# Scan of an RWKV-7 layer: the next front is begun in the chain's first step, its copies, exponents and grams queued behind the merge and the first solutions

## The chip, the cores and the metric

The kernel runs on one core of a Trainium2 chip. The metric is the time of one execution on the device in microseconds (us), the median over several runs. A profiled execution of the same kernel gives the trace.

The engines named below are TensorE (PE, matrix multiplications; PEld is its load of weights), VectorE (DVE), ScalarE (ACT), GpSimd (POOL) and SyncE (SP), which issues the DMAs. Each engine takes its instructions in the order of its own queue and waits where an operand or a buffer isn't ready.

## The reference

Two layers run over 256 context tokens and 512 latent tokens with 1024 features. Layer 0 is windowed attention with an MLP. Layer 1 is an RWKV-7 mixer with an MLP. The change lies in the mixer's scan: for each of 16 heads of 64 features, in both directions, a state of 64 by 64 runs over the tokens; the latent scan begins with the context's last state.

```python
def wkv_scan(r, w, k, v, a, b, s0, reverse):
    def step(s, inp):
        r_t, w_t, k_t, v_t, a_t, b_t = inp
        sa = jnp.einsum('bhvk,bhk->bhv', s, a_t)
        s = s * w_t[:, :, None, :] + sa[..., None] * b_t[:, :, None, :] + v_t[..., None] * k_t[:, :, None, :]
        return s, jnp.einsum('bhvk,bhk->bhv', s, r_t)
...
    _, y_fwd = wkv_scan(r, dec[0], k, v, na, b, s_fwd, False)
    _, y_bwd = wkv_scan(r, dec[1], k, v, na, b, s_bwd, True)
```

## The kernel before

Attention, the two MLPs and the features of the RWKV layer are matrix products split in high and low parts (lines 334 to 366 and their callers); the change doesn't touch them. The features (kk, bp, kp, r, the running sums of the log decay and the gates) are written to memory by tiles of 128 features, and the scan reads them back.

**Items.** `rwkv_scan` cuts the scan into six items (`its`, `plan`). Item 0 is the context of feature tiles 0 to 3 (four tiles, 4 chunks of 64 tokens), items 1 and 2 are the latent tokens of tiles 0, 1 and 2, 3 (two tiles, 8 chunks each); items 3, 4, 5 are the same for tiles 4 to 7. A chunk of one head and one direction is a triangular system of 64 unknowns. Each item goes through these stages:

- **The front**, `prep` (L1153): for each feature tile `fl` and direction `d` it loads the features (`load`, L1184, and the decay sums `cs`, L1197; L1165 to L1174 for a context item), takes two exponents on ScalarE (`en`, L1200, and `cs` in place, L1201; L1177 and L1178 for a context item), and forms the scaled operands by three or four products on DVE (L1213 to L1217). GpSimd copies the decay over a chunk (`PC`, L1218). The buffers: five for the features (`f4`), two for the sums (`cs`, NCS), one for `en` (NEN). Then `grams` (L1223), for four chunks at a time: ScalarE copies the operand into one of two padded tiles (L1235), TensorE makes four products (L1238) in one of two PSUM buffers, DVE masks the result into GM (L1244). One front has eight such grams, called simply grams below.
- **The lanes**, `lanes` (L1278): the diagonal blocks of 32 by 32 are copied from GM to MT (L1284, by `copy`, two on ScalarE at L1263, two on DVE at L1267, by FC), transposed into `lane` (L1285), and inverted by elimination, 30 steps of products and sums on DVE (L1295, L1298). This is a serial chain on one engine.
- **The merge**, `merge` (L1300): the inverse is transposed back twice (L1303 and L1306, both DVE), TensorE makes the off-diagonal block in two stages of 32 by 32 products (L1313, L1321), each in two halves with its evacuation on ScalarE (L1316, L1324), and four copies (L1329, by BC two on ScalarE and two on DVE) put the diagonal blocks in GM.
- **Late work**, `late` (L1247): for a latent item the second half of the grams, for each item the scaling to the chunk's end (L1259) and the transposed operands (`turn`, L1331), done part by part in the steps of the chain before.
- **The chain**, `chain` (L1359): over the chunks in order, in two groups of tiles: x = GM z plus the state's part (L1382, L1385), evacuated to `xsb` on ScalarE (L1390); the solution U = GM xsb (L1397), evacuated to `z` (L1401); the new state (L1412, DVE L1417 for the first, L1423 after); for a latent item the output (L1433, L1437, L1439). After each step `after` loads a later chunk's values, does late work and a piece of the last item's `readout` (L1445).

**Order.** The kernel is written for a scheduler that gives each engine's queue its order at build time: it goes by the order in which the program issues its instructions as a priority, and by the times at which operands and buffers are expected, so that later work can be queued first where earlier work isn't ready. `tc.issue_after(i)` is a fixed order: what the block issues on the engine of instruction `i` stands behind `i` in that engine's queue; other engines aren't bound, and nothing waits on data by it. Before the change, `front(n)` merges item n-1, issues the front of item n with its DVE instructions behind the merge's second transposition (`back`, L1306), and the lanes of item n; then the chain of item n-1 is issued. So the front and the lanes of the next item come ahead of the chain in the program, and beside it in time. The front of the item after that can be loaded, and its first exponents taken, as soon as buffers are free.

Of the kernel before, what the change touches and what calls it, by code (L numbers as in the profile page):

```python
# [11 lines left out]
AF = mybir.ActivationFunctionType  # L12
# [128 lines left out]
LS = (0, 0, 1, 1, 1, 1, 1, 0)  # L141
LC = (0, 2, 4, 4)
NCS = 2
NEN = 1
SQ = ()
LM = ()
LPRE = 0
# [10 lines left out]
RW = {'rt': 'tile'}  # L158
DM = (0, 0, 2, 3, 3, 3, 3, 2)
FC = 'avav'  # L160
BC = 'avav'
TD = ((1, 3),)
NG = 2
NTM = 7
# [6 lines left out]
class K:  # L171
# [909 lines left out]
    def rwkv_scan(self, xsave, osave):  # L1081
# [8 lines left out]
        rl, _ = rconst_layout()  # L1090
# [59 lines left out]
            it.zw = {}  # L1150
            return it

        def prep(it):  # L1153

            it.AR, it.BK, it.GM = ABG[it.set]
            it.PC = sa.tile([P, it.nch, it.nf, 2], F32, tag="pc", bufs=2, name="pc")
# [28 lines left out]
                    src[fl, nm] = t.rearrange("p (c t) -> p c t", t=64)  # L1185

            def part(fl, d):
                if d == 0:
                    load(fl)
                f = it.fts[fl]  # L1190
                b = slice(fl * it.nch, fl * it.nch + it.nch)
                kk, bp, kp = (src[fl, nm] for nm in ("kk", "bp", "kp"))
                inc = slice(1 - d, 65 - d)
                exc = slice(d, 64 + d)
                if it.lat:
                    cs = ftile(it.nch * 65, "cs", NCS, "cs")
                    nc.sync.dma_start(cs, self.fslice(f, f"L{d}", 65 * 4, it.nch * 65))  # L1197
                    cs = cs.rearrange("p (c t) -> p c t", t=65)
                    en = ftile(n, "en", NEN, "en").rearrange("p (c t) -> p c t", t=64)
                    nc.scalar.activation(en, cs[:, :, inc], AF.Exp, scale=self.DEC)  # L1200
                    nc.scalar.activation(cs, cs, AF.Exp, scale=-self.DEC)  # L1201
                else:
                    cs, en = src[fl, d]
                    en = en[:, :, inc]
                ep = cs
                ar, bk = it.AR[:, d, b], it.BK[:, d, b]
                if d == 0:
                    ao, bo, ko = ar[:, :, 0:64], bk[:, :, 0:64], bk[:, :, 64:128]
                    ends = ep[:, :, 64]
                else:  # L1210
                    ao, bo, ko = ar[:, :, 0:64][:, :, ::-1], bk[:, :, 64:128][:, :, ::-1], bk[:, :, 0:64]
                    ends = ep[:, ::-1, 0]
                nc.vector.tensor_tensor(ko, kp, en, ALU.mult)  # L1213
                nc.vector.tensor_tensor(bo, bp, en, ALU.mult)
                nc.vector.tensor_tensor(ao, kk, ep[:, :, exc], ALU.mult)
                if it.lat:
                    nc.vector.tensor_tensor(ar[:, :, 64:128], src[fl, "r"], ep[:, :, inc], ALU.mult)  # L1217
                nc.gpsimd.tensor_scalar(it.PC[:, :, fl, d], ends, 1.0, 0.0, ALU.mult, ALU.add)  # L1218
                grams(it, fl, d, 0)

            return [lambda fl=fl, d=d: part(fl, d) for fl in range(it.nf) for d in range(2)]

# [38 lines left out]
        def copy(eng, o, i):  # L1261
            if eng == "a":
                nc.scalar.activation(o, i, AF.Copy)  # L1263
            elif eng == "p":
                nc.gpsimd.tensor_scalar(o, i, 1.0, 0.0, ALU.mult, ALU.add)
            else:
                nc.vector.tensor_copy(o, i)  # L1267

        def streams(s_):

# [29 lines left out]
        def merge(it):  # L1300
# [2 lines left out]
            nc.vector.transpose(MT.rearrange("p u i -> p i u"), Lt.rearrange("p t s -> p s t"))  # L1303

            DT = dt if it.n else GM[:, 0, :, 64:96]
            it.back = nc.vector.transpose(DT.rearrange("p u t -> p t u"), lane).ins  # L1306
            R = [slice(64 * d, 64 * d + 32) for d in range(2)]
            Q = [slice(64 * d + 32, 64 * d + 64) for d in range(2)]
            for u0 in (0, 16):
# [7 lines left out]
            for u0 in (0, 16):  # L1317
# [3 lines left out]
                        nc.tensor.matmul(ps[R[d], 32 * u:32 * u + 32], MT[Q[d], u0 + u], DT[Q[d], u0 + u],  # L1321
                                         start=True, stop=True, tile_position=(64 * d + 32, 64 * d))
                for d in range(2):
                    nc.scalar.activation(GM[R[d], d, u0:u0 + 16, 32:64], ps[R[d]].rearrange("p (u i) -> p u i", u=16),  # L1324
                                         AF.Copy)
            for j in range(4):
                d, bk_ = j // 2, j % 2
                r = slice(32 * j, 32 * j + 32)
                copy(BC[j], GM[r, d, :, 32 * bk_:32 * bk_ + 32], DT[r])  # L1329

        def turn(it):  # L1331

# [26 lines left out]
        def chain(it, S_, after):  # L1359
# [6 lines left out]
            for i in range(nch):  # L1366
                hpr = tc.high_priority(HP) if HP else ExitStack()
                with hpr:
# [22 lines left out]
                    for g in range(NG):  # L1391
                        hs = range(hg * g, hg * g + hg)
                        gs = slice(hg * g, hg * g + hg)
                        for hd in hs:
                            for d in range(2):
                                o = slice(64 * d, 64 * d + 64)
                                nc.tensor.matmul(UP[o, 64 * hd:64 * hd + 64], GM[:, d, it.cof(i, d) * nh + hd, 0:64], xsb[:, d, hd],  # L1397
                                                 start=True, stop=True, tile_position=(0, 64 * d))
                        for d in range(2):
                            o = slice(64 * d, 64 * d + 64)  # L1400
                            nc.scalar.activation(Z[o, d, gs], UP[o, 64 * hg * g:64 * hg * g + 64 * hg].rearrange(  # L1401
# [147 lines left out]
                return [state[0][:, f:f + 2]]  # L1549
            return [state[f // 2][:, 0:1], state[f // 2][:, 1:2]]  # L1550

        def front(n):
            merge(its[n - 1])

            with tc.issue_after(its[n - 1].back):
                for p in prep(its[n]):
                    p()
            lanes(its[n])
            rest.extend(late(its[n]))
            for _ in range(LPRE):  # L1560
                if rest:
                    rest.pop(0)()

        tail = {}

# [51 lines left out]
            return r  # L1617

        pending, rest = [], []
        front(1)  # L1620
        for n, it in enumerate(its):
            def after(i):
                if i % it.spb == it.spb - 1:
                    lookahead()
                for _ in range(lper if n == len(its) - 1 else (LS if it.lat else LC)[i]):
# [17 lines left out]
            for p in pending + rest:  # L1643
                p()
            rest.clear()
            if n + 2 < len(its):
                front(n + 2)
            elif n + 1 < len(its):
                merge(its[n + 1])
            pending = readout(it) if it.lat else []  # L1650
            if not it.lat:
# [126 lines left out]
```

## Time and profile before

| | us |
|---|---|
| median of 3 runs | 2264.61 (2261.82 to 2271.43) |
| the profiled execution | 2270.0 |
| its span, first to last instruction | 2268.2 |
| from the first merge to the last (L1303) | 1372.5 to 1766.3 |
| from merge to merge | 90.7, 74.8, 75.6, 81.7, 71.0 |
| the last chain, with the output projection beside it | from 1766.3, to about 1852 |

The page gives busy times of the engines over the whole span. The granted clock of TensorE is a mean of 0.944 over it. A row of the timeline has the start in us from the span's first instruction, the duration, the engine, the line, the operation, what it writes and reads, and in brackets the idle time of the engine before it and what ended that. A row with x2 or more stands for that many instructions in a row. The number of a matmul row counts each product twice.

### The profile page before, as it was taken

To read this page: it belongs to the slowest core of one execution; us is meant where nothing else is said; L and a number is where in the kernel's file an instruction comes from. 1 tells how busy PE (TensorE), PEld (TensorE's weight loads), DVE (VectorE), ACT (ScalarE), POOL (GpSimd) and SP (SyncE) were. 2 spreads that over 40 slices of the span, in tenths; PEclk is the share of its full clock that TensorE was granted. 3 is DMA by queue.
4 is the path that set the end of the run, shared out by engine and by line. 5 is a ranking of instruction groups with operands and counts; after the bars stand their busy time and mean duration, and the time that the engine had idled before them with its cause. 6 is when DMAs were issued, how large, how long until landed. Compare 5 with 4: busy or idle time off the path is not lost. (4 is left out here: it accounts for less than half of the span.)

```text
span 2268.2 us, 40460 instructions
## 1 busy us (share of the span) xinstructions
PE 2049.9 (90%) x16208; PEld 1668.3 (74%) x16208; DVE 1320.1 (58%) x2737; ACT 857.2 (38%) x1702; POOL 263.7 (12%) x362
## 2 busy tenths in 40 slices
PE   5989999979999999997979798698869887999999
PEld 4876756868888888885856687586658655787887
DVE  4465565464334343349787665888898657444443
ACT  4344454232111111116454445567647433222121
POOL 0122232010000000001010101000000101101110
PEclk9999999989999999997999898789889898999999
DMA  8344461122122121116146434113311312323322
GB/s 288 102 135 135 138 212 58 56 79 65 61 61 66 56 70 61 53 37 236 63 162 244 135 129 155 35 51 90 95 48 58 128 56 79 103 93 95 96 88 80
DMA packets 115885, 229.67 MB, mean 101 GB/s; under 512 B 12912, under 2 KB 31088, under 8 KB 115312
## 3 DMA queue, kind: packets, MB, share of 16 engines
q1 hardware_dynamic: 115696, 227.08, 31.1%
q8 instruction: 128, 2.10, 0.4%
q14 instruction: 61, 0.50, 0.1%
HBM read 191.80 MB, written 32.60 MB: 99 GB/s over the span
## 5 line engine op out<-in xcount | busy, mean ns | idle before, releaser
L337 DVE TENSOR_TENSOR wlo<-wraw,whi 128x1024 fp32r<-128x1024 f32 (+1 forms) x121 | 134.5, 1120 | 322.6 <-ACT whi L334 169.2
L364 PE MATMUL w_ps<-mhl,whi 128*128 128x512 f32 (+1 forms) x768 | 235.7, 361 | 7.3 <-DVE mhl L317 7.3
L362 PE MATMUL w_ps<-mhh,whi 128*128 128x512 f32 (+1 forms) x768 | 235.1, 361 | 7.1 <-POOL whi L336 3.4
L366 PE MATMUL w_ps<-mhh,wlo 128*128 128x512 f32 (+1 forms) x768 | 235.4, 361 | 5.0 <-DVE wlo L337 5.0
L364 PE MATMUL w_ps<-hid,w2h 128*128 128x512 f32 (+1 forms) x768 | 234.0, 359 | 0.0
L362 PE MATMUL w_ps<-hid,w2h 128*128 128x512 f32 (+1 forms) x768 | 231.4, 355 | 1.6 <-ACT mrelu L689 1.4
L366 PE MATMUL w_ps<-hid,w2l 128*128 128x512 f32 (+1 forms) x768 | 231.1, 355 | 0.0
L334 ACT ACTIVATE w2h<-w2raw 128x512 fp32r<-128x512 f32 x64 | 40.4, 631 | 330.0 <-PE w_ps L364 299.1
L660 DVE SCALAR_TENSOR_TENSOR X<-w_ps,ada,X 128x256 f32<-128x256 f32 (+1 forms) x128 | 73.1, 612 | 137.5 <-PE w_ps L366 137.5
L364 PEld LDWEIGHTS w_ps<-mhl,whi 128*128 128x128 f32 x768 | 127.7, 190 | 33.0 <-DVE mhl L317 9.8
L362 PEld LDWEIGHTS w_ps<-mhh,whi 128*128 128x128 f32 x768 | 127.8, 190 | 31.7 <-POOL whi L336 4.1
L366 PEld LDWEIGHTS w_ps<-mhh,wlo 128*128 128x128 f32 x768 | 127.8, 190 | 31.0 <-DVE wlo L337 8.0
L336 POOL TENSOR_SCALAR whi<-wraw 128x1024 fp32r<-128x1024 f32 (+1 forms) x60 | 69.2, 1154 | 673.2 <-PE w_ps L364 252.6
L366 PEld LDWEIGHTS w_ps<-hid,w2l 128*128 128x128 f32 x768 | 127.4, 189 | 23.3
L362 PEld LDWEIGHTS w_ps<-hid,w2h 128*128 128x128 f32 x768 | 125.5, 188 | 24.8 <-ACT mrelu L689 2.3
L334 ACT ACTIVATE whi<-wraw 128x1024 fp32r<-128x1024 f32 (+1 forms) x61 | 59.1, 968 | 222.7 <-PE w_ps L364 100.8
L364 PEld LDWEIGHTS w_ps<-hid,w2h 128*128 128x128 f32 x768 | 126.6, 188 | 20.7
L689 ACT ACTIVATE mrelu<-w_ps 128x768 f32<-128x768 f32 (+1 forms) x64 | 44.7, 699 | 189.6 <-PE w_ps L366 189.6
L1238 PE MATMUL g_ps<-pad,bk 128*128 128x128 f32 x640 | 98.1, 306 | 6.1 <-DVE gm L1244 2.1
L1238 PEld LDWEIGHTS g_ps<-pad,bk 128*128 128x128 f32 x640 | 86.0, 212 | 15.9 <-ACT pad L1235 7.5
L564 DVE CUSTOM_DVE_ANT_0 sm<-sc_ps,consts,vecs 128x256 f32<-128x256 f32 (+2 forms) x96 | 71.6, 760 | 40.7 <-PE pt_ps L585 21.9
L337 DVE TENSOR_TENSOR w2l<-w2raw,w2h 128x512 fp32r<-128x512 f32 x128 | 89.1, 697 | 4.8 <-ACT w2h L334 4.6
(381 smaller groups left out, 4486.1 us busy)
## 6 DMA issues: line engine op xcount, KB each, us to landing
ada_w<-ada_w SPq DMA_DIRECT2D x160, 256.0 KB, 3.5
wraw<-w SPq DMA_DIRECT2D x64, 512.0 KB, 3.2
w2raw<-w SPq DMA_DIRECT2D x128, 256.0 KB, 2.6
kt<-ada_w SPq DMA_DIRECT2D x32, 256.0 KB, 5.1
feat<-cs SPq DMA_DIRECT2D x16, 390.0 KB, 2.3
cs<-feat SPq DMA_DIRECT2D x24, 260.0 KB, 3.1
wraw<-wq SPq DMA_DIRECT2D x8, 512.0 KB, 3.8
wraw<-wo SPq DMA_DIRECT2D x8, 512.0 KB, 3.2
```

What stands on the lines that cost most here:

```text
L334: nc.scalar.activation(hi, raw, AF.Copy)
L336: nc.gpsimd.tensor_scalar(hi, raw, 1.0, 0.0, ALU.mult, ALU.add)
L337: nc.vector.tensor_tensor(lo, raw, hi.bitcast(F32), ALU.subtract)
L362: nc.tensor.matmul(o, wh, cut(xh, sl), start=start, stop=False)
L364: nc.tensor.matmul(o, wh, cut(xl, sl), start=False, stop=False)
L366: nc.tensor.matmul(o, wl, cut(xh, sl), start=False, stop=stop)
L564: nc.vector.tensor_tensor_reduce(sm[:, :nk], ps[:, :nk], self.c["band"][:, b0:b0 + nk], rs[:, h:h + 1], self.v["sink"][:, hd:hd + 1], ALU. ...
L660: self.nc.vector.scalar_tensor_tensor(self.X[:, m, sl], ps[:, sl], self.ada[:, u, m, s:s + 1], self.X[:, m, sl], ALU.mult, ALU.add)
L689: nc.scalar.activation(r, ps[:, 0:n], AF.Relu)
L1238: nc.tensor.matmul(g[:, P * k:P * k + P], it.BK[:, d, b + k], pv[:, :, k], start=True, stop=True)
```

## The change

The merge of an item is issued alone. The chain's first step follows it, and the next front and lanes are issued in `after(0)`, behind that step in the program. `merge` returns in `merged` its last DVE copy and its last ScalarE evacuation (L1324); the chain keeps its step's last solution (L1397) in `solved`. `prep` gets these three as `behind`: for the first feature tile its products and grams, and for all further tiles everything, are issued after them, each on its own engine (DVE, ScalarE, TensorE). The loads and exponents of the first tile aren't bound. The merge's four copies all go to DVE (`BC`), and stand ahead of the 32 by 32 products in the program. There are two `en` buffers instead of one (`NEN`).

```diff
-NEN = 1
+NEN = 2
...
-BC = 'avav'
+BC = 'vvvv'
...
-        def prep(it):
+        def prep(it, behind=()):
...
             def part(fl, d):
+                order = ExitStack()
+
+                if fl:
+                    for i in behind:
+                        order.enter_context(tc.issue_after(i))
                 if d == 0:
                     load(fl)
...
+                if not fl:
+                    for i in behind:
+                        order.enter_context(tc.issue_after(i))
                 nc.vector.tensor_tensor(ko, kp, en, ALU.mult)
...
                 grams(it, fl, d, 0)
+                order.close()
...
-            it.back = nc.vector.transpose(DT.rearrange("p u t -> p t u"), lane).ins
+            nc.vector.transpose(DT.rearrange("p u t -> p t u"), lane)
+            for j in range(4):
+                d, bk_ = j // 2, j % 2
+                r = slice(32 * j, 32 * j + 32)
+                dve = copy(BC[j], GM[r, d, :, 32 * bk_:32 * bk_ + 32], DT[r])
...
                 for d in range(2):
-                    nc.scalar.activation(GM[R[d], d, u0:u0 + 16, 32:64], ps[R[d]].rearrange("p (u i) -> p u i", u=16),
-                                         AF.Copy)
-            for j in range(4):
-                d, bk_ = j // 2, j % 2
-                r = slice(32 * j, 32 * j + 32)
-                copy(BC[j], GM[r, d, :, 32 * bk_:32 * bk_ + 32], DT[r])
+                    act = nc.scalar.activation(GM[R[d], d, u0:u0 + 16, 32:64], ps[R[d]].rearrange("p (u i) -> p u i", u=16),
+                                               AF.Copy)
+            it.merged = [dve.ins, act.ins]
...
-                                nc.tensor.matmul(UP[o, 64 * hd:64 * hd + 64], GM[:, d, it.cof(i, d) * nh + hd, 0:64], xsb[:, d, hd],
-                                                 start=True, stop=True, tile_position=(0, 64 * d))
+                                it.solved = nc.tensor.matmul(UP[o, 64 * hd:64 * hd + 64], GM[:, d, it.cof(i, d) * nh + hd, 0:64],
+                                                             xsb[:, d, hd], start=True, stop=True, tile_position=(0, 64 * d)).ins
...
-        def front(n):
-            merge(its[n - 1])
-
-            with tc.issue_after(its[n - 1].back):
-                for p in prep(its[n]):
-                    p()
+        def front(n, behind):
+
+            for p in prep(its[n], behind):
+                p()
             lanes(its[n])
             rest.extend(late(its[n]))
...
-        front(1)
+        merge(its[0])
         for n, it in enumerate(its):
             def after(i):
+                if i == 0 and n + 1 < len(its):
+
+                    front(n + 1, it.merged + [it.solved])
...
-            if n + 2 < len(its):
-                front(n + 2)
-            elif n + 1 < len(its):
+            if n + 1 < len(its):
                 merge(its[n + 1])
```

More of the change, by code (lines that the diff above doesn't have):

```diff
@@ L1266, in copy @@
             else:
-                nc.vector.tensor_copy(o, i)
+                return nc.vector.tensor_copy(o, i)
         def streams(s_):
@@ L1550, in carry @@
             return [state[f // 2][:, 0:1], state[f // 2][:, 1:2]]
-        def front(n):
-            merge(its[n - 1])
-            with tc.issue_after(its[n - 1].back):
-                for p in prep(its[n]):
-                    p()
+        def front(n, behind):
+            for p in prep(its[n], behind):
+                p()
             lanes(its[n])
             rest.extend(late(its[n]))
-            for _ in range(LPRE):
-                if rest:
-                    rest.pop(0)()
         tail = {}
```

## The prediction

> **What bounds the kernel now.** I read the page first, to see which engine is full over the whole span.
>
> ```profile
> span 2268.2 us, 40460 instructions
> ## 1 busy us (share of the span) xinstructions
> PE 2049.9 (90%) x16208; PEld 1668.3 (74%) x16208; DVE 1320.1 (58%) x2737; ACT 857.2 (38%) x1702; POOL 263.7 (12%) x362
> ```
>
> TensorE at 90% is an average over the whole program; the change lies in the scan alone. So I cut the scan by stretches, from each transposition that begins a merge (L1303) to the transposition that begins the next elimination (L1285), and from there to the next merge. The first column after the stretch is its length; then come the busy times, DVE third, and PEclk, the granted clock.
>
> ```profile
> core 0: us, PE busy (x) PEld busy (x) DVE busy (x) ACT busy (x) POOL busy (x), PEclk, DMA share, GB/s
> 1463.20:1499.00 35.80, 27.79 (x448) 25.55 (x448) 23.61 (x36) 24.73 (x52) 2.02 (x3) 0.67 0.28 83
> 1499.00:1538.00 39.00, 37.41 (x631) 31.94 (x628) 37.67 (x173) 25.75 (x84) 3.59 (x8) 1.00 0.08 23
> 1538.00:1577.40 39.40, 32.01 (x546) 26.10 (x547) 34.13 (x64) 31.45 (x67) 3.05 (x8) 0.87 0.36 102
> 1577.40:1613.60 36.20, 29.15 (x549) 23.08 (x546) 33.49 (x170) 20.79 (x70) 4.44 (x9) 0.99 0.23 68
> 1613.60:1652.20 38.60, 31.31 (x516) 26.61 (x517) 32.17 (x47) 30.92 (x62) 2.67 (x5) 0.79 0.38 112
> 1652.20:1695.30 43.10, 24.35 (x355) 20.08 (x353) 40.79 (x180) 17.45 (x39) 3.53 (x7) 0.84 0.17 50
> 1695.30:1726.60 31.30, 25.01 (x447) 22.90 (x448) 23.59 (x36) 23.56 (x50) 2.02 (x3) 0.73 0.29 86
> 1726.60:1766.30 39.70, 37.89 (x639) 32.22 (x634) 38.36 (x173) 26.90 (x86) 4.37 (x8) 1.00 0.09 23
> ```
>
> I call the four pairs M1 to M4, after the item that is merged. In the second line of each pair DVE is busy for 97, 93, 95 and 97% of the stretch: the elimination is bound by VectorE. In the first line, the gap, no engine is full; DVE idles 12.2, 5.3, 6.4 and 7.7 us (length less busy), 31.6 us together. A gap has no resource bound, it is a chain of waits. The next view shows DVE in the gap of M1, in order of time (start, duration, then in brackets the idle time before and what ended it).
>
> ```profile
> 1463.18 2.00 DVE L1303 STREAM_TRANSPOSE mt<-lane 128x1024 f32<-128x1024 f32 x1
> ...
> 1469.30 1.41 DVE L1267 COPY gm<-dt 32x1024 f32<-32x1024 f32 x2
> ...
> 1474.45 0.69 DVE L1215 TENSOR_TENSOR ar<-l_kk,cs 128x512 f32<-128x512 f32 x1 [2.15 <-ACT cs L1201]
> ...
> 1480.63 0.69 DVE L1213 TENSOR_TENSOR bk<-l_kp,en 128x512 f32<-128x512 f32 x1 [2.07 <-ACT en L1200]
> ...
> 1483.05 1.28 DVE L1244 TENSOR_TENSOR gm<-g_ps,s_gmask 128x512 f32<-128x512 f32 x2
> ...
> 1496.90 0.69 DVE L1244 TENSOR_TENSOR gm<-g_ps,s_gmask 128x512 f32<-128x512 f32 x1 [0.86 <-PE g_ps L1238]
> ...
> 1498.95 1.97 DVE L1285 STREAM_TRANSPOSE lane<-mt 128x1024 f32<-128x1024 f32 x1
> ```
>
> DVE waits for exponents on ScalarE; then eight masks (L1244) follow one another from 1483.05 to 1496.90, each behind its gram, and the elimination starts 2.05 us after the eighth. So the gap ends when the eighth gram is masked. ScalarE and TensorE in the same gap:
>
> ```profile
> 1466.99 2.12 ACT L1263 ACTIVATE gm<-dt 32x1024 f32<-32x1024 f32 x2 [20.44 <-DVE dt L1306]
> 1469.12 1.19 ACT L1316 ACTIVATE mt<-mg 32x512 f32<-32x512 f32 x2
> ...
> 1476.85 1.19 ACT L1324 ACTIVATE gm<-mg 32x512 f32<-32x512 f32 x2
> ...
> 1479.96 0.63 ACT L1200 ACTIVATE en<-cs 128x512 f32<-128x512 f32 x1 [1.93 <-DMA cs<-feat]
> ...
> 1483.48 0.57 ACT L1390 ACTIVATE xsb<-x_ps 64x128 f32<-64x128 f32 x2
> ```
>
> ```profile
> 1465.33 3.62 PE L1313 MATMUL mg<-mt,gm 32*32 32x32 f32 x128 [18.92 <-DVE mt L1303]
> 1470.37 1.92 PE L1321 MATMUL mg<-dt,mt 32*32 32x32 f32 x64 [1.41 <-ACT mt L1316]
> 1473.81 1.92 PE L1321 MATMUL mg<-dt,mt 32*32 32x32 f32 x64 [1.52 <-ACT mt L1316]
> 1475.65 0.69 PE L1382 MATMUL x_ps<-z,gm 128*64 128x64 f32 x4
> ...
> 1476.70 3.57 PE L1238 MATMUL g_ps<-pad,bk 128*128 128x128 f32 x16
> ...
> 1487.23 0.80 PE L1397 MATMUL u_ps<-xsb,gm 128*64 128x64 f32 x5
> ```
>
> The merge's last evacuation (L1324) ends at 1478.04, 14.9 us after the merge began, because ScalarE puts two block copies (2.12 us) ahead of the first evacuation and exponents and pads between the others. The chain's first solutions (L1397) end at 1488.03, 24.8 us after it. An exponent that waited 1.93 us for its DMA stood ahead of the chain's xsb in ScalarE's queue.
>
> **The change part by part.** Take M as the start of the merge, in M1.
>
> Merge. The two block copies leave ScalarE: 4 copies on DVE at 0.70 us (1.41 for 2) instead of 2, so DVE gets 1.4 us more in each gap, which lies beside DVE's idle time there (5.3 us in the smallest gap). If that were gone it would cost 1.4 us per merge. The evacuations no longer wait for the copies or share with exponents. By the rows: transposed at M+2.0; L1313 takes 1.81 us for each half (3.62 for both), so its halves end at M+4.0 and M+5.8; evacuations of 1.19 us end at 5.2 and 7.0; L1321 at 1.92 us a half ends at 7.7 and 9.6; the last evacuation at M+10.8, instead of M+14.9.
>
> First solutions. x for the two groups: about 1.1 us for the first (the 0.69 us row with the state's part, up to the gram at 1476.70) and 0.7 for the second, to M+12.6; xsb 0.57 us to 13.2; L1397 about 0.6 us (0.80 for five of its matmuls with others between) to M+13.8, instead of 24.8. Nothing on ScalarE stands ahead of them except exponents and pads of the front's first feature tile, which can run earlier.
>
> Second exponent buffer. With NEN at 2 both exponents of the front's first tile, whose sums are loaded ahead, can be taken before the merge. The 2.15 us wait of DVE at 1474.45 goes. What is late next is the second tile: its loads wait for buffers that the first tile's products free. Those products now stand behind four copies, at M+6.6 to about M+11.4 (eight at 0.6 us, since one of 0.69 us overlaps the next), where the row at 1474.45 and one product after it ended at M+12.6 before; the second tile's last exponent so comes about 1 us sooner than its M+16.8, not 10.
>
> Grams. They are now behind the first solutions on TensorE: the first gram can't start before M+13.8, where it started at M+13.5 (1476.70). At half clock one takes 1.79 us (3.57 for two), so its mask starts at M+15.7 instead of M+19.9 in M1. The old one waited on DVE, which was doing the second tile's products. With the later masks following at the old pace, the eighth moves by as much as the first: 4.2 us in M1. For the other gaps I need their first masks, and for M3, a context item with twice the heads, the longer first step (the solutions of one group in the first chain, a context item too):
>
> ```profile
> 1555.85 0.68 DVE L1244 TENSOR_TENSOR gm<-g_ps,s_gmask 128x512 f32<-128x512 f32 x1
> ```
> ```profile
> 1631.70 0.68 DVE L1244 TENSOR_TENSOR gm<-g_ps,s_gmask 128x512 f32<-128x512 f32 x1
> ```
> ```profile
> 1713.79 1.27 DVE L1244 TENSOR_TENSOR gm<-g_ps,s_gmask 128x512 f32<-128x512 f32 x2
> ```
> ```profile
> 1404.13 1.12 PE L1397 MATMUL u_ps<-xsb,gm 128*64 128x64 f32 x16
> ...
> 1405.82 3.19 PE L1238 MATMUL g_ps<-pad,bk 128*128 128x128 f32 x16
> ```
>
> M2: first mask at M+17.8 becomes 15.7, 2.1 us. M4: 18.5 becomes 15.7, 2.8 us. M3: x twice 1.1, an xsb of about 0.8 us (an estimate; 0.57 us is for half its width) and solutions of 1.1 us after M+10.8 end at M+14.9; the mask at 16.8 instead of 18.1, 1.3 us. Sum over the four gaps: 4.2 + 2.1 + 1.3 + 2.8 = 10.4 us.
>
> Chain. It starts 11 us sooner in M1, the elimination 4.2 us sooner, so about one more chain step is done in the gap. The state updates of one step (two groups on a latent item at 0.60 us, as the estimate below takes them; about 2.3 us on the context item with twice the tiles) leave the elimination, where DVE is full, for the gap, where it idles.
>
> ```profile
> 1492.06 0.60 DVE L1423 SCALAR_TENSOR_TENSOR sn<-sn,pc,s_ps 128x128 f32<-128x128 f32 x2 [0.28 <-PE s_ps L1412]
> ```
>
> That is 1.2 us in M1, M2 and M4 and 2.3 in M3: 5.9 us. The bounds are 0 and 5.9; what is left of the idle time after copies and shift (M1 6.6, M2 1.8, M3 3.7, M4 3.5 us) holds all of it, and I take it whole.
>
> First and last merge. In the first gap the gram at 1405.82 already came after the solutions' row at 1404.13: the order asked for is there, I take 0 (bounds 2 us either way, the size of the 2.15 us wait above that a second buffer can remove or another order bring). In the last merge there is no next front; only the copies matter:
>
> ```profile
> 1770.22 2.12 ACT L1263 ACTIVATE gm<-dt 32x1024 f32<-32x1024 f32 x2 [1.61 <-DVE dt L1306]
> 1772.36 0.28 ACT L1439 ACTIVATE yt<-y_ps 128x128 f32<-128x128 f32 x1
> 1772.66 2.40 ACT L1316 ACTIVATE mt<-mg 32x512 f32<-32x512 f32 x4
> ```
>
> At most their 2.12 us, at least nothing, since the read-out's work shares ScalarE there; I take 1.0.
>
> Queues passed: the chain's first step issues no DMA and nothing on GpSimd, so SP and POOL see the front's loads and PC copies in the same order as before, only with the solutions ahead of them on TensorE and ScalarE.
>
> Sum: 10.4 + 5.9 + 1.0 = 17.3 us. The profiled execution took 2270.0 us (span 2268.2 and 1.8 around it) and would take 2252.7; it lay 5.4 us above the median of 2264.61, so on the median's scale the forecast is 2247.3, rounded 2247.
>
> One rule against it: PEclk is 0.67 in the gap of M1 and 1.00 in its elimination, where TensorE is busy all along. The Trainium skill ("TensorE: Matmul & The Clock Gate", What's actually happening) says that the clock is halved after an idle window of some 3.4 us and comes back after as long a busy one. By it, a chain that ends well ahead of its elimination would leave the next merge cold; M2's gap, at 0.87 the best of the four, would lose most. The rows give the price: L1313 at half clock takes 3.62 us, so at most 1.8 us more in M2, which the range holds.
>
> **The rivals.** *First solutions still late (slower).* All grams stand behind one instruction. ScalarE takes its queue in order, and the second tile's exponents, now behind the merge, can land ahead of xsb and wait there for their DMA, as at 1479.96. If the solutions then end at M+20.3, where xsb stood in M1 (1483.48), the first masks come at M+22.2 and, for M3, 23.3: 2.3 + 4.4 + 5.2 + 3.7 = 15.6 us later, less 1.0: 2279. It decides from solutions at about M+16.7, where the mean of the old first masks (18.6) is met. For it: that row, and that the sums' buffers are still two. Against: the order on ScalarE is free to put xsb first.
>
> *Lanes start unmoved (same).* The gap is ended by something other than the first gram: by the second tile's late products (DVE at 1480.63), or in M2 and M3 by the read-out's DVE work. Then only the chain's shift remains, and a part of that: 2 to 6 us, 2261. For it: M2 and M3 idle only 5.3 and 6.4 us, and the copies take 1.4 of it.
>
> *DVE fills the gaps (faster than forecast).* All of 31.6 us idle goes, less 4 times 1.4 of copies: 26 us, and 2 at the last merge: 2237. Against it: the grams' pace still needs ScalarE's pads and two PSUM buffers.
>
> **How the numbers follow.** Forecast 0.50, of which its own range is 2240 to 2258; late solutions 0.17; unmoved 0.25; filled 0.08. 0.5% is 11.3 us, about what a measurement can tell from none here, so the border is 2253.3. Of the forecast's 0.50 about 0.42 lie below it, with most of the filled case and a little of the unmoved one: faster 0.54. Slower (over 2275.9) holds most of the late case and a few of the unmoved: 0.17. Same 0.29. The range 2234 to 2275 leaves out the late case's worse half and the tail of the filled one.
>
> **What would show it.** Right: no L1263 on ScalarE in a merge; L1324 ends near M+11; L1397's first step ends near M+14 with no gram ahead of it; first mask near M+16; gaps of about 31.6, 37.3, 37.3 and 28.5 us; eliminations about 1 us shorter. Wrong: an exponent waiting on a DMA ahead of the first xsb, a first mask later than M+18.6, or a gap whose last wait is a product of the second tile.

## The result, and the profile after

| | before | after |
|---|---|---|
| median | 2263.59 us (4 runs) | 2286.18 us (4 runs, 2283.61 to 2288.82) |
| profiled execution, its span | 2270.0, 2268.2 us | 2284.9, 2283.0 us |
| gaps M1 to M4 (forecast 31.6, 37.3, 37.3, 28.5) | 35.8, 39.4, 38.6, 31.3 | 37.0, 47.0, 43.4, 36.0 |
| eliminations M1 to M4 | 39.1, 36.1, 43.1, 39.7 | 39.1, 35.0, 41.8, 46.4 |
| from the last merge to the end | 501.9 | 495.1 |

The ratio is 1.0093, 95% interval 1.0066 to 1.0120: slower, and above the upper end of the forecast range (2275). Line numbers after are 5 to 13 higher. The stretches of the scan, as in the prediction (first the gap, then the elimination, of M1 to M4; length, then busy times of PE, PEld, DVE, ACT and POOL, the granted clock, DMA):

```profile
PE 2054.7 (90%) x16208; PEld 1676.6 (73%) x16208; DVE 1329.2 (58%) x2749; ACT 844.5 (37%) x1690; POOL 258.9 (11%) x362
```

```profile
core 0: us, PE busy (x) PEld busy (x) DVE busy (x) ACT busy (x) POOL busy (x), PEclk, DMA share, GB/s
1462.20:1499.20 37.00, 29.39 (x484) 26.70 (x484) 25.57 (x40) 22.94 (x53) 0.49 (x2) 0.68 0.27 80
1499.20:1538.30 39.10, 35.91 (x622) 30.68 (x621) 37.06 (x171) 25.79 (x83) 4.59 (x10) 0.98 0.10 25
1538.30:1585.30 47.00, 38.66 (x591) 32.14 (x592) 38.08 (x72) 30.57 (x70) 3.07 (x8) 0.76 0.32 90
1585.30:1620.30 35.00, 25.13 (x471) 20.14 (x469) 31.12 (x163) 19.35 (x63) 3.66 (x8) 0.93 0.19 61
1620.30:1663.70 43.40, 33.12 (x550) 28.44 (x550) 33.86 (x52) 29.65 (x59) 2.37 (x4) 0.74 0.36 105
1663.70:1705.40 41.70, 21.72 (x318) 18.41 (x318) 40.73 (x175) 17.30 (x40) 3.51 (x8) 0.82 0.15 45
1705.40:1741.40 36.00, 29.08 (x492) 26.55 (x492) 25.52 (x40) 22.06 (x53) 0.49 (x2) 0.68 0.24 75
1741.40:1787.90 46.50, 38.97 (x632) 31.53 (x630) 42.87 (x179) 30.92 (x91) 5.37 (x10) 0.98 0.20 67
```

The two profiled executions are 14.8 us apart by their spans (the medians 22.6, as the profiled execution of before lies above its median), so the rows account for 14.8. The page's totals hardly move; the four gaps do: 145.1 us became 163.4, 18.3 more, where 10.4 less were forecast. The other changes nearly cancel: the fourth elimination is 6.7 us longer, and what follows the last merge 6.8 shorter. The groups by line in that elimination name what it took in: 2.7 us of L337, 1.7 of L1476 and 0.8 of L392 on DVE, none of which ran in it before. Work was moved over a border there, which says nothing about the loss.

DVE in the gap of M1, in the changed kernel:

```profile
1466.01 2.80 DVE L1276 COPY gm<-dt 32x1024 f32<-32x1024 f32 x4
...
1479.39 0.69 DVE L1221 TENSOR_TENSOR bk<-l_kp,en 128x512 f32<-128x512 f32 x1 [1.79 <-ACT en L1205]
...
1482.43 0.68 DVE L1225 TENSOR_TENSOR ar<-l_r,cs 128x512 f32<-128x512 f32 x1
...
1485.05 0.69 DVE L1253 TENSOR_TENSOR gm<-g_ps,s_gmask 128x512 f32<-128x512 f32 x1 [1.38 <-PE g_ps L1247]
...
1499.20 1.97 DVE L1294 STREAM_TRANSPOSE lane<-mt 128x1024 f32<-128x1024 f32 x1
```

ScalarE there:

```profile
1471.47 1.19 ACT L1337 ACTIVATE gm<-mg 32x512 f32<-32x512 f32 x2 [0.51 <-PE mg L1334]
1472.68 1.73 ACT L1244 ACTIVATE pad<-ar 64x256 f32<-64x256 f32 x4
1474.43 0.63 ACT L1205 ACTIVATE en<-cs 128x512 f32<-128x512 f32 x1
1475.09 0.57 ACT L1400 ACTIVATE xsb<-x_ps 64x128 f32<-64x128 f32 x2
1478.72 0.63 ACT L1205 ACTIVATE en<-cs 128x512 f32<-128x512 f32 x1 [3.07 <-DMA cs<-feat]
1479.26 1.15 ACT L1206 ACTIVATE cs<-cs 128x520 f32<-128x520 f32 x2
1480.43 0.56 ACT L1400 ACTIVATE xsb<-x_ps 64x128 f32<-64x128 f32 x2
```

TensorE there:

```profile
1475.41 0.47 PE L1407 MATMUL u_ps<-xsb,gm 128*64 128x64 f32 x2 [1.57 <-ACT xsb L1400]
...
1476.68 0.42 PE L1395 MATMUL x_ps<-sn,ar 128*64 128x128 f32 x1
...
1481.04 0.58 PE L1392 MATMUL x_ps<-z,gm 128*64 128x64 f32 x3 [3.51 <-ACT xsb L1400]
...
1482.14 0.54 PE L1407 MATMUL u_ps<-xsb,gm 128*64 128x64 f32 x6
...
1482.93 3.34 PE L1247 MATMUL g_ps<-pad,bk 128*128 128x128 f32 x15
```

Take 1462.2 as M. The merge came out as worked out: its last evacuation ends at M+10.5 (10.8 forecast), and the first solution starts at M+13.2. The second group's x stands behind that one in TensorE's queue and is ready at 1477.10 (the L1395 row at 1476.68). Its xsb could follow there, but on ScalarE it stands behind an exponent that waits 3.07 us for its DMA. It runs at 1480.43, the last solution ends at M+20.6, the first gram starts at M+20.7 and the first mask at M+22.9, where M+15.7 was forecast and M+19.9 was the old value. All grams stand behind that one solution.

The DVE lines show a second thing: until 1483.1 (M+20.9) DVE does the second tile's products, which wait for the same exponent, and its queue has them ahead of the first mask. So a mask has two chains to wait for, and in M1 they end 2 us apart. In M2 it is this second one that ends last. The rows are of M2's gap (M is 1538.3), for TensorE, ScalarE and DVE:

```profile
1556.06 2.77 PE L1247 MATMUL g_ps<-pad,bk 128*128 128x128 f32 x16
```

```profile
1558.06 0.64 ACT L1177 ACTIVATE en<-cs 128x520 f32<-128x520 f32 x1 [1.53 <-DMA cs<-feat]
```

```profile
1558.73 0.42 DVE L1221 TENSOR_TENSOR bk<-l_kp,en 128x256 f32<-128x256 f32 x1 [1.94 <-ACT en L1177]
...
1561.35 0.69 DVE L1253 TENSOR_TENSOR gm<-g_ps,s_gmask 128x512 f32<-128x512 f32 x1
```

The two grams of the x16 row end at 1558.8; the first mask comes 2.5 us later, behind products of the front's last tile, whose exponent waited for its load.

### The profile page after: what moved, and what is told of

Read it like the earlier page. It is cut to its first block, busy times and chain, and to the rows that moved or that the text cites. A ratio compares the mean times of both kernels' runs of the same rounds, so it can differ in the third digit from the quotient of the medians.

```text
span 2283.0 us, 40448 instructions
## 1 busy us (share of the span) xinstructions
PE 2054.7 (90%) x16208; PEld 1676.6 (73%) x16208; DVE 1329.2 (58%) x2749; ACT 844.5 (37%) x1690; POOL 258.9 (11%) x362
## 3 DMA queue, kind: packets, MB, share of 16 engines
q1 hardware_dynamic: 115696, 227.08, 30.5%
## 5 line engine op out<-in xcount | busy, mean ns | idle before, releaser
L337 DVE TENSOR_TENSOR wlo<-wraw,whi 128x1024 fp32r<-128x1024 f32 (+1 forms) x121 | 135.0, 1123 | 320.0 <-ACT whi L334 168.3
L366 PEld LDWEIGHTS w_ps<-hid,w2l 128*128 128x128 f32 x768 | 127.4, 189 | 23.3
L362 PEld LDWEIGHTS w_ps<-hid,w2h 128*128 128x128 f32 x768 | 125.5, 188 | 22.8 <-ACT mrelu L689 0.8
L364 PEld LDWEIGHTS w_ps<-hid,w2h 128*128 128x128 f32 x768 | 126.5, 188 | 20.9
L564 DVE CUSTOM_DVE_ANT_0 sm<-sc_ps,consts,vecs 128x256 f32<-128x256 f32 (+2 forms) x96 | 71.6, 760 | 39.1 <-PE pt_ps L585 20.2
L336 POOL TENSOR_SCALAR w2h<-w2raw 128x512 fp32r<-128x512 f32 x64 | 42.5, 664 | 426.1 <-PE w_ps L364 326.2
```

Of the source, the lines that this page charges most:

```text
L336: nc.gpsimd.tensor_scalar(hi, raw, 1.0, 0.0, ALU.mult, ALU.add)
L337: nc.vector.tensor_tensor(lo, raw, hi.bitcast(F32), ALU.subtract)
L362: nc.tensor.matmul(o, wh, cut(xh, sl), start=start, stop=False)
L364: nc.tensor.matmul(o, wh, cut(xl, sl), start=False, stop=False)
L366: nc.tensor.matmul(o, wl, cut(xh, sl), start=False, stop=stop)
L564: nc.vector.tensor_tensor_reduce(sm[:, :nk], ps[:, :nk], self.c["band"][:, b0:b0 + nk], rs[:, h:h + 1], self.v["sink"][:, hd:hd + 1], ALU. ...
```

## The experiments

All ratios are to the kernel before, with their 95% intervals. Gaps, first masks and "solved" (the end of the first step's last solution, after M) are of the profiled execution, M1 to M4; "sums" are the four gaps, the four eliminations, and the time from the last merge to the end. "Bindings" are the fixed orders of the change: on DVE behind the merge's last copy, on ScalarE behind its last evacuation, on TensorE behind the last first solution.

| kernel | ratio | gaps | solved | first mask | sums |
|---|---|---|---|---|---|
| before | 1 | 35.8 39.4 38.6 31.3 | 28.7 25.4 27.8 24.2 | 19.9 17.8 18.1 18.5 | 145, 158, 502 |
| copies alone | 0.9959 [0.9946, 0.9973] | 31.0 37.2 37.9 30.5 | 23.9 21.8 25.4 23.4 | 14.8 14.6 15.6 16.0 | 137, 156, 500 |
| second `en` alone | 0.9976 [0.9961, 0.9992] | 31.8 38.0 36.2 28.4 | 26.2 25.8 28.6 23.7 | 16.4 16.4 15.7 15.9 | 134, 161, 499 |
| both | 0.9987 [0.9973, 1.0002] | 30.4 40.6 37.4 30.0 | 22.8 23.6 28.4 22.9 | 16.5 16.8 16.9 17.0 | 138, 158, 498 |
| + the move, DVE bound | 1.0010 [0.9996, 1.0025] | 31.6 40.2 36.9 30.1 | 23.4 22.8 25.0 22.0 | 16.0 17.5 15.8 15.8 | 139, 170, 496 |
| + ScalarE bound | 1.0044 [1.0025, 1.0063] | 33.6 41.0 39.9 33.2 | 23.3 17.5 23.4 21.8 | 18.8 14.8 18.2 17.5 | 148, 166, 495 |
| DVE, TensorE bound | 1.0076 [1.0050, 1.0102] | 37.1 43.2 42.0 34.4 | 19.8 20.8 20.3 19.8 | 22.1 24.1 24.8 21.0 | 157, 161, 496 |
| after (all three) | 1.0093 [1.0066, 1.0120] | 37.0 47.0 43.4 36.0 | 20.6 17.6 20.8 20.0 | 22.9 23.0 24.5 22.3 | 163, 162, 495 |
| none bound | 1.0084 [1.0053, 1.0116] | 25.4 34.6 28.7 26.5 | 18.6 22.9 19.9 19.7 | 12.1 15.1 11.6 12.7 | 115, 195, 499 |

### xsb ahead of the second tile

```diff
-                            nc.scalar.activation(xsb[o, d, gs], xv[o], AF.Copy)
+                            it.xdone = nc.scalar.activation(xsb[o, d, gs], xv[o], AF.Copy).ins
-                    front(n + 1, it.merged + [it.solved])
+                    front(n + 1, [it.merged[0], it.xdone, it.solved])
```

> The changed kernel, but on ScalarE the front's bound instructions (all pads, and the second tile's exponents) stand behind the last xsb of the chain's first step instead of behind the merge's last evacuation. Queue theory (the grams stand behind the first solutions, and these behind an exponent that waits for its DMA on ScalarE): the first solutions end near M+14 instead of M+20, the first mask comes near M+17 in M1 and M4, the gaps of M1, M3 and M4 get 4 to 6 us shorter, the time falls to 2258 to 2270 us. Copies theory (four copies on VectorE push the products and so the loads and grams later): first solutions earlier, gaps as in the changed kernel within 1 us, 2280 us or more. Priority theory (the chain's step ahead of the front in the program is what costs): 2280 us or more.

Measured: 2284.81 us, ratio 1.0089 [1.0072, 1.0106]; gaps 36.2, 48.3, 46.8, 35.3; solved at M+18.9, 18.8, 20.2, 19.1. The time is that of the changed kernel: the 2258 to 2270 us of the queue theory did not come. The two other theories both gave 2280 or more, and this run alone doesn't tell them apart. ScalarE and TensorE in its M1 gap (M is 1461.2):

```profile
1474.96 0.56 ACT L1400 ACTIVATE xsb<-x_ps 64x128 f32<-64x128 f32 x2 [1.48 <-PE x_ps L1395]
1475.54 1.69 ACT L1244 ACTIVATE pad<-ar 64x256 f32<-64x256 f32 x4
1477.26 1.15 ACT L1205 ACTIVATE en<-cs 128x512 f32<-128x512 f32 x2
1478.43 0.57 ACT L1411 ACTIVATE z<-u_ps 64x128 f32<-64x128 f32 x2
```

```profile
1478.75 0.48 PE L1422 MATMUL s_ps<-z,bk 128*64 128x64 f32 x4 [2.74 <-ACT z L1411]
...
1479.45 0.64 PE L1407 MATMUL u_ps<-xsb,gm 128*64 128x64 f32 x8
```

The second xsb now ends at M+14.3, 4.6 us before the last solution does. But TensorE's queue has the first group's state products ahead of the second group's solutions, they wait for the z copy, and z stands behind pads and exponents. The lateness moved one instruction on.

### The whole first step ahead of the second tile

```diff
-                            nc.scalar.activation(Z[o, d, gs], UP[...]..., AF.Copy)
+                            it.zdone = nc.scalar.activation(Z[o, d, gs], UP[...]..., AF.Copy).ins
-                    front(n + 1, it.merged + [it.solved])
+                    front(n + 1, [it.merged[0], it.zdone, it.solved])
```

> The changed kernel with one edit: on ScalarE the second tile's work waits for the last z copy of the chain's first step, in place of the merge's last evacuation; the bindings on VectorE and TensorE stay. Theory 'late solutions': the price of TensorE's binding is the time at which the last first solution ends; with the whole first step ahead on ScalarE it ends at about M+14.5 instead of M+17.6 to 20.8, the first gram begins at M+14.6, the first mask comes at about M+17 to 18 instead of 22.3 to 24.5, the gaps shrink by 4 to 5 us each and the time is about 2267 (ratio 1.001 to 1.003). Rival 'the exponents': the second tile's sums are only read from M+15 on, its exponents end at M+18 or later and VectorE waits for them with its products, so that the grams come sooner and the masks of the second tile later: gaps as in the changed kernel, 2280 to 2288 (ratio 1.007 to 1.011).

Measured: 2289.51 us, ratio 1.0111 [1.0092, 1.0130]; gaps 39.2, 48.1, 50.0, 37.1; solved at M+15.3, 15.8, 17.6, 15.9; first masks M+23.7, 23.4, 25.6, 24.3. The solutions now end 1.5 to 2.7 us after the times that the prediction had for them (M+13.8, and 14.9 in M3), and the masks are later than in the changed kernel. DVE in its M1 gap (M is 1455.8), where the first two grams ran from 1472.60 to 1474.65:

```profile
1474.10 0.69 DVE L1221 TENSOR_TENSOR bk<-l_kp,en 128x512 f32<-128x512 f32 x1 [2.26 <-ACT en L1205]
...
1478.84 0.68 DVE L1225 TENSOR_TENSOR ar<-l_r,cs 128x512 f32<-128x512 f32 x1
1479.44 1.28 DVE L1253 TENSOR_TENSOR gm<-g_ps,s_gmask 128x512 f32<-128x512 f32 x2
```

The masks stand behind the second tile's products, and those wait for exponents that now come after the whole step on ScalarE. So the rival put down for this run holds in its mechanism, with a time a little above its 2280 to 2288, and the theory that late solutions are the whole price falls: with the solutions early, the second of the two chains takes their place. This run doesn't move one chain alone, though: the same edit holds the second tile's first exponent back from M+12.2 to M+17.7.

### Grams behind the first group's solutions

The second tile's work on TensorE, and the first tile's grams, wait for the last solution of the first group in place of the second. (`it.solved` is now a list, empty at first.)

```diff
-                                it.solved = nc.tensor.matmul(...).ins
+                                it.solved[g:] = [nc.tensor.matmul(...).ins]
-                    front(n + 1, it.merged + [it.solved])
+                    front(n + 1, it.merged + it.solved[:1])
```

> The changed kernel with one edit: the second tile's work on TensorE waits for the last solution of the first group of heads, no longer of the second group. Theory 'late solutions': the first group's solutions end at about M+14 to 15, as its x copies are not held by the sum load; the grams start there, five to six us sooner than in the changed kernel, and the first mask comes at M+17 to 18; the second group's solutions still come late and now also stand among the grams, so the time falls most of the way to that of the kernel without TensorE's binding (2272): 2270 to 2276, ratio 1.003 to 1.006. Rival 'the hold itself': any gram behind a solution costs the same, because the grams then share TensorE with the state products; 2282 to 2288.

Measured: 2273.53 us, ratio 1.0044 [1.0030, 1.0059]; gaps 33.8, 44.0, 38.6, 32.4; first grams at M+15.0, 15.5, 16.6, 15.0; solved at M+19.4, 20.0, 20.8, 19.8. The time forecast for "late solutions" came; of the masks only M2's came at the M+17 to 18 expected, the others at M+20.4, 21.7 and 20.6. TensorE and DVE in M1 (M is 1460.9):

```profile
1475.24 0.80 PE L1408 MATMUL u_ps<-xsb,gm 128*64 128x64 f32 x5
1475.97 3.02 PE L1248 MATMUL g_ps<-pad,bk 128*128 128x128 f32 x16
1479.31 0.45 PE L1393 MATMUL x_ps<-z,gm 128*64 128x64 f32 x4 [0.32 <-ACT xsb L1401]
```

```profile
1477.66 0.69 DVE L1222 TENSOR_TENSOR bk<-l_kp,en 128x512 f32<-128x512 f32 x1 [0.94 <-ACT en L1206]
...
1481.30 1.28 DVE L1254 TENSOR_TENSOR gm<-g_ps,s_gmask 128x512 f32<-128x512 f32 x2
```

In the changed kernel TensorE idled 3.51 us before 1481.04, waiting for the second xsb. Here two grams fill most of that wait, and two masks follow one another at once. The kernel is 12.7 us faster than the changed one (2286.18 less 2273.53, in different sets of runs) though its solutions are as late. What cost was work held behind a late instruction that it doesn't need. The rival, that any gram behind a solution costs the same (2282 to 2288 us), falls. And here, with the exponents as early as in the changed kernel, the grams of M1 start 5.7 us sooner and the first mask comes only 2.5 us sooner: it again stands behind the second tile's last product.

### No binding on TensorE

```diff
-                    front(n + 1, it.merged + [it.solved])
+                    front(n + 1, it.merged)
```

> The changed kernel without the first solution among the three instructions that bind the front: the grams are free of it on TensorE, everything else stays. Queue theory: the first gram starts near M+13 instead of M+20, the first mask near M+17 to 20, the solutions may stay near M+20; the gaps shrink by 3 to 5 us each, 2265 to 2275 us. Copies theory: grams and gaps as in the changed kernel, 2280 us or more. Priority theory: 2280 us or more, with the first gram early and the later ones late.

Measured: 2272.02 us, ratio 1.0044 [1.0025, 1.0063]. First grams at M+10.9 to 11.9, and the gaps 15.7 us shorter than after, of which 4.0 come back in the eliminations; the time is in the 2265 to 2275 us of the queue theory. Setting all grams free brings no more than putting them behind the first group.

### No binding on ScalarE

```diff
-                    front(n + 1, it.merged + [it.solved])
+                    front(n + 1, [it.merged[0], it.solved])
```

> The changed kernel without ScalarE's binding: products behind the copies, grams behind the first solutions. Queue theory: the grams are still held to the end of the first solutions, near M+20, first masks near M+22, 2275 to 2290 us. If ScalarE's binding was the cause: 2250 to 2265 us.

Measured: 2281.41 us, ratio 1.0076 [1.0050, 1.0102]. Beside the changed kernel (1.0093) the intervals overlap: with TensorE bound, ScalarE's binding isn't told from nothing. The time is in the queue theory's 2275 to 2290 us.

### Only DVE bound

```diff
-                    front(n + 1, it.merged + [it.solved])
+                    front(n + 1, it.merged[:1])
```

> The changed kernel with one of the three bindings, VectorE's (products behind the merge's copies). If the bindings of ScalarE and TensorE cost: 2248 to 2262 us. If the place in the program costs: 2268 us or more. Against the kernel without any binding it tells what VectorE's costs: by the rows at most 1.4 us a merge.

Measured: 2266.83 us, ratio 1.0010 [0.9996, 1.0025], between the two ranges put down (up to 2262, from 2268), so neither theory is the whole of it. The first masks are at M+16.0, 17.5, 15.8, 15.8 and the gaps 31.6, 40.2, 36.9, 30.1: close to the forecast of the prediction in M1 and M3, 2.9 and 1.6 us longer in M2 and M4, without the solutions being early (solved at M+22.0 to 25.0). But the eliminations are 12 us longer than before, M3's 46.8 and M4's 47.8, which takes up what the gaps (6 us shorter) and the stretch after the last merge (6 us shorter) give. Between this kernel and the one with TensorE bound as well the step is 1.0010 to 1.0076, about 15 us; to the one with ScalarE bound as well 1.0010 to 1.0044, about 8 us. The two together make 1.0093, 19 us.

### No binding at all

```diff
-                    front(n + 1, it.merged + [it.solved])
+                    front(n + 1, [])
```

> The changed kernel with the front in the chain's first step and no binding at all: nothing of the front is put behind the merge or the solutions. If the place in the program alone costs (the chain's step has priority over the front): first solutions near M+14, first mask near M+19, 2268 us or more. If the bindings cost: 2248 to 2262 us, near the kernel with the two small parts alone.

Measured: 2282.35 us, ratio 1.0084 [1.0053, 1.0116]. The time is in the range for a costly place in the program (2268 or more), but not for its reason: the first masks came at M+11.6 to 15.1, not near M+19, and the solutions at M+18.6 to 22.9, not near M+14. M2's gap and elimination:

```profile
1539.10:1573.70 34.60, 30.93 (x506) 25.23 (x506) 30.67 (x51) 23.98 (x50) 0.31 (x2) 0.79 0.25 72
1573.70:1634.50 60.80, 36.86 (x574) 26.57 (x574) 55.14 (x203) 33.52 (x93) 7.24 (x12) 0.79 0.41 123
```

The gaps are the shortest of all, 30 us less than before, and the eliminations 37 us longer: products of the front after the next run among the elimination's steps, as this one on DVE in M2:

```profile
1597.31 0.68 DVE L1222 TENSOR_TENSOR bk<-l_bp,en 128x512 f32<-128x512 f32 x1
```

So DVE's binding saves about 17 us here (1.0084 to 1.0010), where it was expected to cost up to 1.4 us a merge. A short gap alone is no gain: the sum of gap and elimination is. Over M1 to M4 that sum is 310 us here and 309 with DVE bound. Most of what DVE's binding saves lies in the stretch from the first merge to the second, which the table leaves out: 101.5 us here, 90.6 with DVE bound.

### The small parts by themselves

The copies: `BC` and the merge's new order in the kernel before, with nothing else of the change.

```diff
-BC = 'avav'
+BC = 'vvvv'
```

> The kernel before with one part of the change: the merge's four copies on VectorE, ahead of the 32 by 32 products in the program. Queue theory: the merge ends near M+12 instead of M+14.9, the order of front and chain is that of before, 2258 to 2268 us. Copies theory: the second tile's products and the gaps come 1 to 3 us later each, 2270 us or more. Priority theory: as the queue theory.

Measured: 2254.45 us, ratio 0.9959 [0.9946, 0.9973], faster than both kernels, and than the 2258 to 2268 us expected; M1's merge ends at M+13.2 instead of 14.8 (M+12 was expected), and its first mask comes at M+14.8.

The second exponent buffer in the kernel before:

```diff
-NEN = 1
+NEN = 2
```

> The kernel before with one part of the change: two buffers for the exponent instead of one. Every theory: the 2.15 us waits of VectorE for ScalarE's second exponent go, the gaps shrink by up to 2 us each, 2254 to 2264 us; if the wait is only handed on to the second tile's loads, no change, 2260 to 2266 us.

Measured: 2257.62 us, ratio 0.9976 [0.9961, 0.9992], inside the 2254 to 2264 us expected. And the two together:

> The kernel before with both small parts of the change (the four copies on VectorE, two exponent buffers) and without the move: front and lanes are issued ahead of the chain, as before. Queue theory (the loss is the move's: grams, pads and exponents behind the chain's first step, in queues that wait): the two gains add, 8.7 + 5.5 us, 2246 to 2253 us, so the move alone costs about 35 us. Parts theory (the parts cancel each other or harm together): 2256 us or more.

Measured: 2259.39 us, ratio 0.9987 [0.9973, 1.0002]. The 2246 to 2253 us of gains that add did not come: of 9 us and 5 us there remain about 3. DVE in M1 with both (M is 1459.6):

```profile
1463.18 0.72 DVE L1213 TENSOR_TENSOR bk<-l_kp,en 128x512 f32<-128x512 f32 x1
...
1467.96 2.79 DVE L1267 COPY gm<-dt 32x1024 f32<-32x1024 f32 x4
```

and with the copies alone (M is 1461.4):

```profile
1465.02 0.69 DVE L1213 TENSOR_TENSOR bk<-l_kp,en 128x512 f32<-128x512 f32 x1
...
1467.39 2.79 DVE L1267 COPY gm<-dt 32x1024 f32<-32x1024 f32 x4
```

With both exponents of the first tile taken early, eight products, not four, run ahead of the merge's copies, and the copies start at M+8.4 instead of M+6.0. Whether this is the whole of what is lost, no run shows.

### A third buffer of sums

The copies alone, with a third buffer for the running sums:

```diff
-BC = 'avav'
+BC = 'vvvv'
-NCS = 2
+NCS = 3
```

> The kernel before with the merge's four copies on VectorE and ahead (as in the run of the copies alone, ratio 0.996), and with a third buffer for the running sums. Theory: the second tile's load and exponents, which come some 5 us after the buffer comes free, end part of the gap; with a third buffer the load is issued a tile earlier and the gaps shrink by 1 to 3 us each: 2243 to 2250, ratio 0.991 to 0.994. Rival: the masks and products on VectorE fill the gap already (VectorE is idle 4 to 8 us of it, elsewhere than before the products); the time stays that of the copies alone, 2252 to 2256, ratio 0.995 to 0.997. Rival on the other side: earlier products run ahead of the merge's copies, as with the second buffer of exponents, and the gain of the copies goes: 2258 to 2262.

Measured: 2255.93 us, ratio 0.9962 [0.9950, 0.9973], the same as without the buffer. The waits of DVE for exponents are gone from M1 (idle 5.6 us in place of 6.1) and the gaps are 30.2, 41.9, 36.8, 28.9: three a little shorter, M2's 4.7 longer. The first rival holds. Three buffers of sums together with two of exponents weren't tried, so what the changed kernel would do without its late loads stays open.

## Why the prediction was wrong

**Merge:** right. M+10.5 for 10.8, and the copies are a gain by themselves.

**First solutions:** here the prediction failed. They were to end at M+13.8 (14.9 in M3), and they ended at M+17.6 to 20.8. "Nothing on ScalarE stands ahead of them except exponents and pads of the front's first feature tile" held for the first group alone. Of the 6.8 us in M1, 2.3 come from x: the second group's was ready at M+14.9, not M+12.6, because on TensorE it stands behind the first of the first group's solutions, and these waited for their own xsb. Another 3.3 come from the second group's xsb, behind the second tile's exponent that waited 3.07 us for its DMA (2.23 and 2.44 in M3 and M4). The last 1.2 are solutions that took 1.8 us among other products, not 0.6. In M2 no such wait for a load stood ahead of the xsb, and the solutions still ended at M+17.6.

The slower rival described the wait on ScalarE, with solutions at M+20.3, masks at M+22.2 and 2279 us; the masks came at M+22.3 to 24.5 and the time at 2286. It was given 0.17, "the order on ScalarE is free to put xsb first", though the change binds xsb to nothing and the trace of before already had an exponent waiting ahead of it.

The 24.8 us that the prediction set against M+13.8 were misread, too: 1488.03 is the end of the first group's solutions. The second group's last one in the kernel before is this row, which ends at M+28.7:

```profile
1491.66 0.22 PE L1397 MATMUL u_ps<-xsb,gm 128*64 128x64 f32 x1
```

So the change did bring the last solution of M1 forward, by 8 us. Before, no gram was bound to it: the first gram started at M+13.5, far ahead of it.

**Grams:** "the first gram can't start before M+13.8" was the right rule with the wrong input. But the step from there to the mask would have failed too: the prediction followed one chain to the first mask, solutions to gram to mask, and left out that DVE takes the second tile's products ahead of the masks. It had worked out that their exponents come "about 1 us sooner than its M+16.8, not 10", and drew nothing from it. In M1 the last product after the change ended at M+20.9; and with the grams behind the first group, when they started at M+15.0, the first mask still came at M+20.4. With TensorE's binding alone gone, a mask as early as the forecast M+15.7 came in M2 only (14.8); with ScalarE's gone as well, they came at M+16.0, 15.8 and 15.8 in M1, M3 and M4.

**Sum over the gaps:** 10.4 us less became 18.3 more. That a gap moves by as much as its first mask held in the sum alone: the first masks came 3.0, 5.2, 6.4 and 3.8 us later than before, 18.4 in all, and the gaps grew by 1.2, 7.6, 4.8 and 4.7. The runs put the loss on the two bindings, which together cost some 19 us (1.0010 to 1.0093): TensorE's the larger part, about 15 us alone, because grams stood behind a solution that they don't need.

**Second buffer and copies:** costed as if they added. Alone the copies are worth 9 us and the buffer 5, together about 3.

**Chain:** 5.9 us were to leave the eliminations. M1 to M3 gave 2.4 (0.0, 1.1, 1.3), M4 nothing that can be separated from the work that came into it. Without the two bindings the eliminations of M3 and M4 grew by 3.7 and 8.1 us. The place in the program itself (both parts, against both with the move and DVE's binding: 0.9987 and 1.0010) is 5 us slower at best guess, and the intervals overlap; DVE's binding differs between the two as well (behind the second transposition, behind the last copy).

**Clock:** the price put on the merge's first products was about right. TensorE at M2's merge before, and after:

```profile
1540.24 2.21 PE L1313 MATMUL mg<-mt,gm 32*32 32x32 f32 x128
```

```profile
1540.48 3.46 PE L1326 MATMUL mg<-mt,gm 32*32 32x32 f32 x122 [4.41 <-DVE mt L1312]
```

TensorE had idled 4.41 us ahead of the merge, and its first products took at least 1.25 us more (at most 1.8 were put down); the granted clock was 0.50 while they ran, 1.00 before, and over the gap it fell from 0.87 to 0.76. The trace agrees with the rule of the Trainium skill ("TensorE: Matmul & The Clock Gate", What's actually happening) in that the clock is halved around an idle stretch and comes back later, but not in the lengths of some 3.4 us each. The mean clock over the 4.38 us from 1536.10, when TensorE was idle, is 0.61; with levels of 1.00 and 0.50 it was halved about 1 us after the last product, and it stayed at 0.50 through 6.7 us of unbroken 32 by 32 products (1540.48 to 1547.20) and on to about 1557.5. M2's gap did lose most, 7.6 us, as that argument had it; but its first mask stood behind DVE's products and not behind a gram. What the longer stretch at half clock adds to that gap no run separates.

## What to carry to other kernels

An order fixed behind an instruction costs whatever makes that instruction late, so ask what stands ahead of it in every queue that leads to it, and whether the held work needs it at all. Follow every chain that meets at the operation which ends a stage, not the one that the change moves: speeding up one can hand the end to the next, as it did here. And time the small parts of a change alone; here one of them (the copies, ratio 0.9959) beat the whole and the kernel before.

## What the runs showed of the hardware

A load took longer among others. The second tile's sums of 260 KB were issued at 1473.81 in M1, the last but one of a run of six loads, and by the trace their exponent, which waited for them alone, began at 1478.72. SyncE's row of the issue:

```profile
1473.81 0.32 SPq L1202 DMA_DIRECT2D cs<-feat  x1
```

That is 4.9 us, where the page of the same run has a median of 3.4 us from issue to landing for these loads. Of the six, the four feature loads took longer the later they were issued, from issue to landing: 2.7, 3.6 and 4.8 us for those before it, 5.1 us for the one after it. This wait is what the late xsb stood behind.
